# Order of evictions, forms and bank numbers in a one-core encoder layer built from seven-product blocks

## The chip, the core and the metric

The kernel runs on one core of a Trainium2 chip. The metric is device time of one execution in microseconds (us). A compared time is the median of several runs. One further execution is profiled; the traces quoted below come from it.

## The reference

One encoder layer in fp32 on 256 tokens of width 2048: a half-weighted SwiGLU feed-forward (FFN, hidden width 5632), a mixer of two attentions, a second such FFN, a gated per-token embedding and a final RMSNorm.

```python
h = h + 0.5 * swiglu(rmsnorm(h, ffn1_norm), ffn1_w_gate, ffn1_w_up, ffn1_w_down)
z = rmsnorm(h, mix_norm) @ w_in           # q|k|v, MLA latents, rope key, gate_a, gate_b
merged = sigmoid(gate_a) * (NA2D(q, k, v) @ w_branch_a) + sigmoid(gate_b) * (MLA(...) @ w_branch_b)
h = h + merged @ w_out
h = h + 0.5 * swiglu(rmsnorm(h, ffn2_norm), ffn2_w_gate, ffn2_w_up, ffn2_w_down)
h = h + sigmoid(rmsnorm(h, pl_norm) @ w_pl_gate) * (p @ w_pl)
return rmsnorm(h, final_norm)
```

## The kernel before, in words

**Products.** Every fp32 operand is held as two parts, hi (rounded by a cast on ACT) and lo (the rest, a subtraction on DVE). `split` (lines 90 and 91) makes them; `triple` (lines 95 to 97) multiplies them with three matmuls on TensorE (PE): x_lo by hi, x_hi by hi, x_hi by lo. A row "L95" or "L96" thus uses the hi tile of a weight, "L97" the lo tile.

**Granules.** All matrix products are cut into granules, kept in the list `grans` in the order in which PE works them off. The loop at the end of the file takes each granule g in turn. It first calls `convert()`, which starts coming granules' weight loads and splits as long as tiles W0 to W5 are free (a granule of an FFN needs two of them, one of a unit one), then writes the granule's matmuls, then runs the tasks that `at(d, fn)` put down for this step d granules ago, and then frees the granule's W tiles. The framework adds the semaphores; the order on each engine is the order in which the code is written (`manual_schedule`). Raw weights land in three buffers R0 to R2 by DMAs that SyncE issues.

**Units.** The mixer and the embedding are made of `Unit`s: ordinary products that add up in two PSUM banks out of B0 to B3, handed out in turn by `acc_bank` with the counter `turn["acc"]`, and evacuated by `evac`. A unit granule has 12 matmuls.

**Blocks.** The FFNs' products are `Block`s. Each computes two outputs for two token tiles (c11, c12, c21, c22) with seven products in place of eight wherever the 2x2 scheme is used (granules i in `SEVEN` = {2, 4, 6}, each in a first half `SevenA` of 9 matmuls and a second half `SevenB` of 12) and with plain products elsewhere (`Plain`, 24 matmuls). Eight banks collect partial sums q1 to q8; q1 lies in B0, q6 in B1, q7 in B2, q3 in B3, q2 in B4, q4 in B5, q5 in B6, q8 in B7 (`add`, line 218). Gate and up projections make one block per 512 hidden columns with 11 granules (i = 0 to 7); each of the three parts of the down projection makes two blocks. There are 33 blocks.

**A block's end.** The last granule is always a plain one. One step after the last `SevenB`, `early` (lines 187 to 195) gathers q1, q5, q6 and q7 on ACT and DVE. At the last granule the loop calls `late`'s two functions: `first` adds q2 and q4 (lines 201 and 202), then `convert()` writes the next weight split, then `rest` adds q8 and q3 (lines 205 and 206) and calls `done`: Silu and a product (lines 537 and 538) after a gate and up block, an addition to h (line 548, or line 550's DMA) after a down block. The next block's first granule is plain: its matmuls write B4, B5, B7 and B3 in this order, six each.

**Forms.** The activations that a block multiplies are made by `make_form`: four transposes on PE into a side bank (`bank`: B0 to B2 in turn inside the FFNs), then for a plain chunk a cast on ACT (line 385) and a subtraction on DVE that reads the bank (line 394), and for a chunk in `SEVEN` a copy to Z on ACT, four sums on DVE (line 357) and a split of 7 x 128 columns (lines 90 and 91, tile H or X, "128x896" in the profile). `hidden_forms` makes two chunks one granule after each gate and up block, `new_forms` two at each quarter of the mixer's last product. Next to the sixteen pairs in which the first chunk is in `SEVEN`, the FFNs have pairs of two plain chunks.

**Norms.** `next_stat` puts down the squares of a quarter of h (line 454, two instructions on ACT and their accumulator reads). After the last part's first down block, `added` puts them down 2 and 3 granules later.

Of the kernel before, what the change touches and what calls it, by code (L numbers as in the profile page):

```python
# [11 lines left out]
ALU = mybir.AluOpType  # L12
# [9 lines left out]
SEVEN = {2, 4, 6}  # L22
# [5 lines left out]
def encoder_kernel(ctx, tc, x, p, ffn1_norm, ffn1_w_gate, ffn1_w_up, ffn1_w_down, mix_norm, w_in,  # L28
# [11 lines left out]
    V, S, G, PE = nc.vector, nc.scalar, nc.gpsimd, nc.tensor  # L40
# [13 lines left out]
    def piece(tag, shape, dt=F32):  # L54
        return mem.tile(shape, dt, tag=tag, name=nm(tag))
# [5 lines left out]
    turn = {"acc": 0, "side": 0, "raw": 0}  # L61
# [24 lines left out]
    def at(d, fn):  # L86
        tasks.setdefault(step[0] + d, []).append(fn)

    def split(hi, lo, r):
        S.copy(hi, r)  # L90
        V.tensor_tensor(out=lo, in0=r, in1=hi.bitcast(F32), op=ALU.subtract)  # L91
# [22 lines left out]
    class Granule:  # L114
# [25 lines left out]
        def matmuls(self):  # L140
            u, k0, nk, hi, lo = self.u, self.k0, self.nk, self.hi, self.lo
            if k0 == 0:
                u.ps = [acc_bank() for _ in range(2 if u.N == 512 else 1)]
            ps = u.ps
            for k in range(nk):
                kt = k0 + k
                if u.N < 512:
                    xh, xl = u.xop(kt)
                    o = ps[0][0:u.N, 0:T]
                    PE.matmul(o, hi[:, k, :], xl, start=(kt == 0), stop=False)  # L150
                    PE.matmul(o, hi[:, k, :], xh, start=False, stop=False)
                    PE.matmul(o, lo[:, k, :], xh, start=False, stop=(kt == u.K - 1))
                    continue
                one = u.by_token and kt >= 4
                for t in range(1 if one else 2):
                    triple(ps[t], u.xtile(kt, t), hi[:, k, :], lo[:, k, :], kt == 0, kt == u.K - 1)
                if one:
                    u.kept.append((kt, hi[:, k, :], lo[:, k, :]))
            if k0 + nk == u.K:
                if not u.by_token:  # L160
                    u.evac(ps)
                    return
                u.evac(ps, 0)
                for kt, a, b in u.kept:
                    triple(ps[1], u.xtile(kt, 1), a, b, False, kt == u.K - 1)
                u.evac(ps, 1)

    def unit(*a, **k):
        Unit(*a, **k)
# [4 lines left out]
    class Block:  # L174
# [22 lines left out]
        def late(self):  # L197
            q = self.q

            def first():  # L200
                V.tensor_tensor(out=self.u, in0=q[2], in1=self.u, op=ALU.add)  # L201
                V.tensor_tensor(out=self.v, in0=q[4], in1=self.v, op=ALU.add)  # L202

            def rest():
                V.tensor_tensor(out=self.c, in0=q[8], in1=self.c, op=ALU.add)  # L205
                V.tensor_tensor(out=self.w, in0=q[3], in1=self.w, op=ALU.add)  # L206
                self.done(self.u, self.w, self.v, self.c)
            return first, rest

# [23 lines left out]
    class Plain(Pair):  # L233
# [6 lines left out]
        def matmuls(self):  # L240
            b, hi, lo = self.blk, self.hi, self.lo
            seven_on[0] = True
            f = b.form(self.i)
            for n, ws, fs in ((2, (0, 1), (1, 2)), (4, (0, 1), (0, 3)), (8, (3, 2), (0, 3)), (3, (3, 2), (1, 2))):
                for k in range(2):
                    b.add(n, f(fs[k]), hi[:, ws[k], :], lo[:, ws[k], :], self.end and k == 1)
            if self.end:
                return b.late()

    class SevenA(Pair):  # L250
# [51 lines left out]
    for nme, g in (("ffn1", ffn1_norm), ("mix", mix_norm), ("ffn2", ffn2_norm), ("pl", pl_norm),  # L302
                   ("qa", q_a_norm), ("kva", kv_a_norm)):
        n = g.shape[-1] // P
# [58 lines left out]
    def plain_tiles(src, i):  # L363

        ps = bank()
        for j, (k, t) in enumerate(((0, 1), (0, 0), (1, 0), (1, 1))):
            PE.transpose(ps[:, j * P:j * P + P], src(t, 2 * i + k), ident)  # L367
        return ps
# [6 lines left out]
    def place(where, i):  # L375
        tag, half = where[i]
        if i in SEVEN:
            return piece(tag, [P, 2, 8, P], F32R)
        if half == 0:
            shared[tag] = piece(tag, [P, 2, 2, 4, P], F32R)  # L380
        return shared[tag][:, half]
# [19 lines left out]
    def make_form(where, i, j, src, gc=None):  # L401

        ps = plain_tiles(src, j)
        f = place(where, i)
        if i not in SEVEN:
            plain_form(f, ps, gc)
            return f
        z = piece("Z", [P, 8, P])
        scaled(z[:, 0:4, :].rearrange("p a b -> p (a b)"), ps, gc)
        sums(z[:, 0:4, :], z[:, 4:8, :])  # L410
        split(f[:, 0, 1:8], f[:, 1, 1:8], z[:, 1:8, :])
        return f

    def new_forms(n, gname):
        for i in (2 * n, 2 * n + 1):
            forms[i] = make_form(XPLACE, i, i, h_tile, gcol[gname] + 2 * i)

    zs = []
# [86 lines left out]
    def next_stat(phase, n, d):  # L505
        def f():
            stat_chunk(phase, n)
            if n == 3:
                stat_done(phase)
        at(d, f)  # L510
# [5 lines left out]
    def tmps(tag):  # L516
        return [tmp.tile([P, 512], F32, tag=tag, name=nm(tag)) for _ in range(2)]


    def ffn(phase, wg, wu, wd, nxt):  # L520
        hidden = {}

        def hidden_forms(c, a, d):
            m = c % 4

            def tr(j):
                i = 2 * m + j
                hidden[i] = make_form(HPLACE, i, j, lambda t, kt: a[t][:, kt * P:kt * P + P])
            for j in range(2):
                at(d[j], lambda j=j: tr(j))  # L530

        def gated(c):
            def done(c11, c12, c21, c22):
                r, rh = rstd[phase], half[phase]
                s = tmps("s")
                for t, (g, u) in enumerate(((c11, c12), (c21, c22))):
                    S.activation(s[t], g, AF.Silu, scale=r[:, t:t + 1])  # L537
                    V.scalar_tensor_tensor(out=u, in0=u, scalar=rh[:, t:t + 1], in1=s[t],  # L538
                                           op0=ALU.mult, op1=ALU.mult)
                hidden_forms(c, [c12, c22], (1, 1))  # L540
            return done

        def added(n, final):
            def done(c11, c12, c21, c22):
                for k, t, o in ((n, 0, c11), (n, 1, c21), (n + 1, 0, c12), (n + 1, 1, c22)):
                    hs = h[:, t, k * 512:k * 512 + 512]
                    if final:
                        V.tensor_tensor(out=hs, in0=hs, in1=o, op=ALU.add)
                    else:
                        G.dma_start(hs, o, accum_op=ALU.add)  # L550
                if not final:
                    return
                if n == 0:
                    at(1, lambda: new_xT(0, nxt))
                    at(1, lambda: new_xT(1, nxt, (0,)))
                    at(2, lambda: new_xT(1, nxt, (1,)))
                    next_stat(nxt, 0, 2)
                    next_stat(nxt, 1, 3)
                else:
                    at(2, lambda: new_xT(2, nxt))  # L560
                    at(3, lambda: new_xT(3, nxt))
                    next_stat(nxt, 2, 4)
                    next_stat(nxt, 3, 5)
            return done

        hold = {}

        def gate_evac(ps):
            at(4, lambda: gate_late(ps))

        def gate_late(ps):
            r = rstd[phase]
            hold["a"] = tmps("t")
            for t in range(2):
                S.activation(hold["a"][t], ps[t], AF.Silu, scale=r[:, t:t + 1])

        def up_evac(ps):
            rh = half[phase]
            a = hold.pop("a")
            for t in range(2):  # L580
                V.scalar_tensor_tensor(out=a[t], in0=ps[t], scalar=rh[:, t:t + 1], in1=a[t],
                                       op0=ALU.mult, op1=ALU.mult)
            hidden_forms(0, a, (1, 2))

        for c0, c1 in PARTS:
            for c in range(c0, c1):
                if grans:
                    Block([rows(wg, c * 512), rows(wu, c * 512)], form_of(forms), 8, gated(c))
                else:
                    unit(rows(wg, 0), 16, 512, None, gate_evac, xtile=first_tile)  # L590
                    unit(rows(wu, 0), 16, 512, None, up_evac, xtile=first_tile)
            part = wd[c0 * 512:c1 * 512]
            for n in (0, 2):
                Block([rows(part, n * 512), rows(part, n * 512 + 512)], form_of(hidden), 2 * (c1 - c0),
                      added(n, c1 == NC_FF))
# [610 lines left out]
```

## Time and profile before

| what | value |
|---|---|
| median of 3 runs | 2188.25 us (2185.91 to 2188.34) |
| profiled execution | 2186.35 us |
| its span, first to last instruction | 2184.6 us |
| PE busy | 2153.1 us (99%) |
| DVE busy | 1720.2 us (79%) |
| ACT busy | 1128.9 us (52%) |
| mean granted TensorE clock | 0.997 of full speed |

An instruction's row in the timeline has its start and its duration in us, its engine and line, what it writes and reads, and in brackets how long the engine idled before it and who ended that. "PE" is a matmul, "PEld" the load of its stationary operand, which runs beside the matmul before it. Matmuls overlap: one is 0.39 us long but the next starts 0.23 us after it, so a delay shorter than 0.16 us shows no idle time.

### The profile page before, as it was taken

How to read it: one execution, taken by the hardware profiler on the slowest of the kernel's cores; microseconds unless marked ns; L12 is line 12 of the kernel's file. 1: busy time of each engine (PE TensorE's matmuls, PEld its weight loads, DVE VectorE, ACT ScalarE, POOL GpSimd, SP SyncE). 2: the span in 40 equal slices, each digit the busy share in tenths (PEclk: the TensorE clock that was granted, in tenths of full speed). 3: DMA queues.
4: the chain of work that ended last, by engine and by line, in shares of the span. 5: the costliest groups of instructions: out<-in, count | busy, mean ns of one | idle time of the engine just before them, and what ended most of it. 6: DMA issues, size and time to landing. Idle time of an engine off the chain costs nothing.

```text
span 2184.6 us, 25377 instructions
## 1 busy us (share of the span) xinstructions
PE 2153.1 (99%) x9693; PEld 1771.4 (81%) x9693; DVE 1720.2 (79%) x1856; ACT 1128.9 (52%) x1172; POOL 64.6 (3%) x73
## 2 busy tenths in 40 slices
PE   9999999999999999999999999999999999999998
PEld 8878888888887888888888888788888878887786
DVE  6899889998999855555655556999889998899865
ACT  6455555554555554445544445555455554555553
POOL 0000000000000000230000000000000000000000
PEclk9999999999999999999999999999999999999999
DMA  7556765567655554574455555556676647755653
GB/s 260 185 188 196 233 193 193 200 211 226 204 195 177 176 190 145 155 212 157 160 194 184 192 192 174 193 193 209 201 218 201 211 160 233 230 186 189 211 171 128
DMA packets 218026, 421.99 MB, mean 193 GB/s; under 512 B 13576, under 2 KB 14160, under 8 KB 217776
## 3 DMA queue, kind: packets, MB, share of 16 engines
q1 hardware_dynamic: 212048, 408.46, 56.3%
q0 software_dynamic: 5824, 11.89, 3.0%
q8 instruction: 76, 1.25, 0.2%
q14 instruction: 46, 0.38, 0.0%
q10 hardware_dynamic: 32, 0.01, 0.0%
HBM read 409.83 MB, written 2.10 MB: 189 GB/s over the span
## 4 chain that ended last, share of the span: by engine, by line
PE 81%; DVE 13%; issue 3%; ACT 3%; DMA 1%; DVEq 0%; POOL 0%; ACTq 0%; POOLq 0%
PE B L97 26%; PE B L95 26%; PE B L96 25%; DVE W L91 6%; ACT W L90 2%; DVE t L202 1%; DVE pt L205 1%; DVE R L257 1%; DVE Z L357 1%; DMA R<-in_w_in_dram 1%; DVE pt L538 1%; PE B L775 1%; PE B L343 1%; PE B L367 1%; DVE R L259 1%
## 5 line engine op out<-in xcount | busy, mean ns | idle before, releaser
L91 DVE TENSOR_TENSOR W<-R,W 128x1024 fp32r<-128x1024 f32 (+2 forms) x697 | 1065.2, 1546 | 321.2 <-ACT W L90 319.2
L90 ACT CAST W<-R 128x1024 fp32r<-128x1024 f32 (+2 forms) x697 | 904.4, 1310 | 709.8 <-DVE R L257 279.2
L95 PE MATMUL B<-W,X 128*128 128x512 f32 x2113 | 835.8, 396 | 8.1 <-DVE pt L206 4.2
L97 PE MATMUL B<-W,X 128*128 128x512 f32 x2113 | 825.0, 390 | 4.1 <-DVE W L91 4.1
L96 PE MATMUL B<-W,X 128*128 128x512 f32 x2113 | 823.7, 390 | 0.0
L95 PEld LDWEIGHTS B<-W,X 128*128 128x128 f32 x2113 | 397.4, 188 | 97.6 <-DVE pt L205 9.5
L97 PEld LDWEIGHTS B<-W,X 128*128 128x128 f32 x2113 | 397.2, 188 | 91.5 <-DVE W L91 7.9
L96 PEld LDWEIGHTS B<-W,X 128*128 128x128 f32 x2113 | 397.6, 188 | 80.3
L95 PE MATMUL B<-W,H 128*128 128x512 f32 x800 | 314.4, 393 | 2.7 <-DVE H L394 1.6
L97 PE MATMUL B<-W,H 128*128 128x512 f32 x800 | 312.3, 390 | 3.5 <-DVE W L91 3.5
L96 PE MATMUL B<-W,H 128*128 128x512 f32 x800 | 311.6, 389 | 0.0
L95 PEld LDWEIGHTS B<-W,H 128*128 128x128 f32 x800 | 150.2, 188 | 39.1 <-DVE pt L205 6.1
L97 PEld LDWEIGHTS B<-W,H 128*128 128x128 f32 x800 | 150.2, 188 | 37.5 <-DVE W L91 6.0
L96 PEld LDWEIGHTS B<-W,H 128*128 128x128 f32 x800 | 150.3, 188 | 30.4
L257 DVE TENSOR_TENSOR R<-R 128x1024 f32<-128x1024 f32 x95 | 116.4, 1225 | 3.3
L260 DVE TENSOR_TENSOR R<-R 128x512 f32<-128x512 f32 x95 | 65.8, 692 | 3.2
L259 DVE TENSOR_TENSOR R<-R 128x512 f32<-128x512 f32 x95 | 65.8, 692 | 3.3
L550 POOL DMA_DIRECT2D h<-t x16 | 14.1, 1018 | 1410.5 <-DVE t L201 1186.6
L385 ACT COPY Z<-B 128x512 f32<-128x512 f32 x16 | 9.4, 586 | 67.4 <-PE B L367 67.4
L90 ACT CAST H<-Z 128x896 fp32r<-128x896 f32 x16 | 15.1, 943 | 53.9 <-DVE Z L357 53.9
L537 ACT ACTIVATE s<-t,sm 128x512 f32<-128x512 f32 x42 | 28.1, 717 | 26.4 <-DVE t L201 26.4
L385 ACT CAST H<-B 128x512 fp32r<-128x512 f32 x28 | 15.8, 584 | 30.7 <-PE B L367 30.7
(207 smaller groups left out, 1047.1 us busy)
## 6 DMA issues: line engine op xcount, KB each, us to landing
R<-in_ffn_w_down_dram SPq DMA_DIRECT2D x176, 512.0 KB, 5.4
R<-in_ffn_w_gate_dram SPq DMA_DIRECT2D x170, 512.0 KB, 3.7
R<-in_ffn_w_up_dram SPq DMA_DIRECT2D x168, 512.0 KB, 4.9
R<-in_w_in_dram SPq DMA_DIRECT2D x64, 1024.0 KB, 5.2
R<-in_w_out_dram SPq DMA_DIRECT2D x16, 1024.0 KB, 5.0
R<-in_w_pl_gate_dram SPq DMA_DIRECT2D x16, 1024.0 KB, 5.1
R<-in_w_branch_a_dram SPq DMA_DIRECT2D x8, 1024.0 KB, 4.9
R<-in_w_branch_b_dram SPq DMA_DIRECT2D x8, 1024.0 KB, 5.0
```

Source lines behind the costliest of these rows:

```text
L90: S.copy(hi, r)
L91: V.tensor_tensor(out=lo, in0=r, in1=hi.bitcast(F32), op=ALU.subtract)
L95: PE.matmul(o, xl, hi, start=start, stop=False)
L96: PE.matmul(o, xh, hi, start=False, stop=False)
L97: PE.matmul(o, xh, lo, start=False, stop=stop)
L202: V.tensor_tensor(out=self.v, in0=q[4], in1=self.v, op=ALU.add)
L205: V.tensor_tensor(out=self.c, in0=q[8], in1=self.c, op=ALU.add)
L257: V.tensor_tensor(out=raw[:, 0:4:3, :], in0=raw[:, 0:3:2, :], in1=raw[:, 3:4, :].to_broadcast([P, 2, 512]), op=ALU.add)
L259: V.tensor_tensor(out=raw[:, 2, :], in0=raw[:, 0, :], in1=raw[:, 2, :], op=ALU.add)
L260: V.tensor_tensor(out=raw[:, 1, :], in0=raw[:, 2, :], in1=raw[:, 1, :], op=ALU.add)
L385: S.copy(o, ps)
L537: S.activation(s[t], g, AF.Silu, scale=r[:, t:t + 1])
```

## The change

In `late`, `first` now adds all four sums, q8 and q3 too, ahead of `convert()`, and `rest` only calls `done`. When the last granule of a block is written, the bank counter for units goes back to 0. In `make_form`, the split of a `SEVEN` chunk's form is put off by one granule. In `new_forms` and in `hidden_forms`, the plain chunk of a pair comes first. In `added`, the squares of the first two quarters of h move from 2 and 3 granules to 5 and 6 granules after the last part's first down block.

```diff
             def first():
                 V.tensor_tensor(out=self.u, in0=q[2], in1=self.u, op=ALU.add)
                 V.tensor_tensor(out=self.v, in0=q[4], in1=self.v, op=ALU.add)
-
-            def rest():
                 V.tensor_tensor(out=self.c, in0=q[8], in1=self.c, op=ALU.add)
                 V.tensor_tensor(out=self.w, in0=q[3], in1=self.w, op=ALU.add)
+
+            def rest():
                 self.done(self.u, self.w, self.v, self.c)
             return first, rest
...
             if self.end:
+                turn["acc"] = 0
                 return b.late()
...
         sums(z[:, 0:4, :], z[:, 4:8, :])
-        split(f[:, 0, 1:8], f[:, 1, 1:8], z[:, 1:8, :])
+        at(1, lambda: split(f[:, 0, 1:8], f[:, 1, 1:8], z[:, 1:8, :]))
         return f
...
-        for i in (2 * n, 2 * n + 1):
+        for i in sorted((2 * n, 2 * n + 1), key=lambda i: i in SEVEN):
...
-            for j in range(2):
+            for j in sorted((0, 1), key=lambda j: 2 * m + j in SEVEN):
                 at(d[j], lambda j=j: tr(j))
...
-                    next_stat(nxt, 0, 2)
-                    next_stat(nxt, 1, 3)
+                    next_stat(nxt, 0, 5)
+                    next_stat(nxt, 1, 6)
```

No instruction is added or taken away on any engine. On DVE, this is the end of the seventh gate and up block of FFN 1 (near 400 us in the trace of before) and the two granules behind it, before; B4, B5, B7, B3 are q2, q4, q8, q3, R raw weights, W their split, Z and H forms:

```order
L201 TENSOR_TENSOR t_445_2992<-B4_408_2713,t_445_2992 128x512
L202 TENSOR_TENSOR t_446_2993<-B5_409_2720,t_446_2993 128x512
L91 TENSOR_TENSOR W3_451_3007<-R0_449_3003,W2_450_3006 128x2048
L205 TENSOR_TENSOR pt_448_2995<-B7_410_2727,pt_448_2995 128x512
L206 TENSOR_TENSOR pt_447_2994<-B3_411_2734,pt_447_2994 128x512
...
L260 TENSOR_TENSOR R1_454_3018<-R1_454_3018 128x512
L357 TENSOR_TENSOR Z_463_3062<-Z_463_3062 128x128 x4
L91 TENSOR_TENSOR H2_462_3061<-Z_463_3062,H2_462_3061 128x896
L394 TENSOR_TENSOR H4_416_2760<-B2_464_3070,H4_416_2760 128x512
L91 TENSOR_TENSOR W1_466_3078<-R1_454_3018,W0_465_3077 128x2x512
L91 TENSOR_TENSOR W1_466_3078<-R1_454_3018,W0_465_3077 128x1024
L91 TENSOR_TENSOR W3_469_3111<-R2_467_3107,W2_468_3110 128x2048
```

The same stretch of DVE in the changed kernel, where most line numbers are one higher:

```order
L201 TENSOR_TENSOR t_445_2992<-B4_408_2713,t_445_2992 128x512
L202 TENSOR_TENSOR t_446_2993<-B5_409_2720,t_446_2993 128x512
L203 TENSOR_TENSOR pt_448_2995<-B7_410_2727,pt_448_2995 128x512
L204 TENSOR_TENSOR pt_447_2994<-B3_411_2734,pt_447_2994 128x512
L91 TENSOR_TENSOR W3_451_3009<-R0_449_3005,W2_450_3008 128x2048
...
L261 TENSOR_TENSOR R1_454_3018<-R1_454_3018 128x512
L395 TENSOR_TENSOR H4_413_2746<-B1_461_3056,H4_413_2746 128x512
L358 TENSOR_TENSOR Z_464_3069<-Z_464_3069 128x128 x4
L91 TENSOR_TENSOR W1_466_3076<-R1_454_3018,W0_465_3075 128x2x512
L91 TENSOR_TENSOR W1_466_3076<-R1_454_3018,W0_465_3075 128x1024
L91 TENSOR_TENSOR H2_463_3068<-Z_464_3069,H2_463_3068 128x896
L91 TENSOR_TENSOR W3_469_3111<-R2_467_3107,W2_468_3110 128x2048
```

The two sums that read B7 and B3 moved ahead of one weight split; the plain form's subtraction (H4) moved ahead of the sums in Z; the split of H2 moved behind the two of W1 but still stands ahead of that of W3.

On PE, this is the first unit of the embedding (its weights are in W1) right behind the last block's last matmul, before:

```order
L97 MATMUL B3_2257_14761<-W5_2286_14921,H4_2175_14228 128x512
L95 MATMUL B3_2297_15002<-W1_2288_14935,X0_2258_14768 128x512
L96 MATMUL B3_2297_15002<-W1_2288_14935,X0_2258_14768 128x512
L97 MATMUL B3_2297_15002<-W1_2288_14935,X0_2258_14768 128x512
L95 MATMUL B0_2298_15003<-W1_2288_14935,X0_2258_14768 128x512
```

And in the changed kernel:

```order
L97 MATMUL B3_2257_14761<-W5_2284_14917,H4_2172_14214 128x512
L95 MATMUL B0_2297_15002<-W1_2288_14935,X0_2258_14768 128x512
L96 MATMUL B0_2297_15002<-W1_2288_14935,X0_2258_14768 128x512
L97 MATMUL B0_2297_15002<-W1_2288_14935,X0_2258_14768 128x512
L95 MATMUL B1_2298_15003<-W1_2288_14935,X0_2258_14768 128x512
```

The unit's two banks were B3 and B0 and are now B0 and B1. PE's order is otherwise the same, but for the two chunks of a pair, whose transposes change places.

## The prediction, made before the changed kernel was run

> **What bounds the kernel now.** I read the page first, then what PE waited for, then PE's timeline around one wait of each kind, then the DVE and ACT rows that those waits hang on.
>
> ```profile
> span 2184.6 us, 25377 instructions
> ...
> PE 2153.1 (99%) x9693; PEld 1771.4 (81%) x9693; DVE 1720.2 (79%) x1856; ACT 1128.9 (52%) x1172; POOL 64.6 (3%) x73
> ```
>
> PE is busy for 2153.1 of 2184.6 us, so it sets the time, and an edit that moves no PE work can only take waits out of it. The view of PE's waits names them:
>
> ```profile
> PE B L97 <- DVE W L91: 7.6, 15, 1.0
> PE B L95 <- DVE pt L206: 4.2, 1, 4.2
> PE B L95 <- DVE H L394: 4.1, 5, 0.9
> ```
>
> That is 16 us. It isn't all, because matmuls overlap. PE's timeline just behind a block's end:
>
> ```profile
> 402.32 0.39 PE L97 MATMUL B<-W,X 128*128 128x512 f32 x1
> 402.79 0.50 PE L95 MATMUL B<-W,X 128*128 128x512 f32 x1
> 403.13 0.40 PE L96 MATMUL B<-W,X 128*128 128x512 f32 x1
> 403.37 0.40 PE L97 MATMUL B<-W,X 128*128 128x512 f32 x1
> ```
>
> No idle time is shown, yet three steps take 403.37 - 402.32 = 1.05 us where three of 0.23 take 0.69: 0.36 us are lost. The view of line 205 (q8's sum, once per block), under who waited for it (us, times):
>
> ```profile
>   PEld B L95: 15.6, 31
> ```
>
> So 31 of 33 block ends hold up the weight load of the first matmul into q8's bank. The Trainium skill ("Perfetto Trace Analysis", the note at its head) calls matmul busy time a bad metric because matmuls are pipelined. This trace agrees: by busy time and idle rows 16 us could go, by starts twice as much (below).
>
> **Part 1, four sums in a row: 31 waits go.** DVE at the same block's end:
>
> ```profile
> 398.65 0.68 DVE L201 TENSOR_TENSOR t<-B,t 128x512 f32<-128x512 f32 x1
> 399.25 0.68 DVE L202 TENSOR_TENSOR t<-B,t 128x512 f32<-128x512 f32 x1
> 399.85 2.28 DVE L91 TENSOR_TENSOR W<-R,W 128x2048 fp32r<-128x2048 f32 x1
> 402.05 0.69 DVE L205 TENSOR_TENSOR pt<-B,pt 128x512 f32<-128x512 f32 x1
> ```
>
> The weight split of 2.28 us stands between the four sums, of which two in a row are 0.60 apart; L206 follows L205 like that. L205 ends at 402.74 and PE goes on at 402.79. With the split behind, q8's sum starts at 399.85 and ends at 400.53, 2 us before PE wants its bank (402.55), and q3's ends at 401.13. Gain: 31 x 0.36 = 11.2 us. The price: the split starts 1.20 later and ends at 403.33 in place of 402.13. Its first use on PE:
>
> ```profile
> 407.03 0.39 PE L97 MATMUL B<-W,X 128*128 128x512 f32 x1
> ```
>
> 4.9 us of cover before, 407.03 - 0.36 - 403.33 = 3.3 after: nothing. Behind it on DVE stand L538's products, which need Silu and wait for the same total of DVE work as before, so the transposes and `done` come no later. The raw buffer comes free 1.2 us later; SyncE's load into it serves a split three granules on, over 10 us later, and a load takes about 5. Nothing there. POOL's DMA additions (line 550) stay behind the same split.
>
> **Part 2, forms.** All sixteen hidden pairs with a `SEVEN` chunk end in one wait on PE each, eleven like this and five for line 394:
>
> ```profile
> 412.04 0.39 PE L95 MATMUL B<-W,X 128*128 128x512 f32 x1
> ...
> 417.03 0.39 PE L96 MATMUL B<-W,X 128*128 128x512 f32 x1
> 417.77 0.50 PE L97 MATMUL B<-W,X 128*128 128x512 f32 x1 [0.35 <-DVE W L91]
> 418.11 0.40 PE L95 MATMUL B<-W,X 128*128 128x512 f32 x1
> 418.35 0.40 PE L96 MATMUL B<-W,X 128*128 128x512 f32 x1
> ```
>
> Three steps from 417.03 take 1.32 in place of 0.69: a shown idle of 0.35 costs 0.63, so idle plus 0.28. The 15 waits for L91 are these eleven, three long ones (part 3) and one at the kernel's start, which stays; (7.6 - 0.4 - 3.0) / 11 gives 0.38 each, so 11 x 0.65 = 7.2 us. The five for L394, whose row stands above, cost 4.1 + 5 x 0.28 = 5.5 us. Both hang on this stretch of DVE and ACT:
>
> ```profile
> 409.15 1.01 DVE L357 TENSOR_TENSOR Z<-Z 128x128 f32<-128x128 f32 x4
> 411.23 1.09 DVE L91 TENSOR_TENSOR H<-Z,H 128x896 fp32r<-128x896 f32 x1 [1.06 <-ACT H L90]
> 412.23 0.69 DVE L394 TENSOR_TENSOR H<-B,H 128x512 fp32r<-128x512 f32 x1
> 412.83 2.35 DVE L91 TENSOR_TENSOR W<-R,W 128x1024 fp32r<-128x1024 f32 x2
> 415.42 3.96 DVE L91 TENSOR_TENSOR W<-R,W 128x2048 fp32r<-128x2048 f32 x2 [0.23 <-ACT W L90]
> ```
>
> ```profile
> 410.25 0.94 ACT L90 CAST H<-Z 128x896 fp32r<-128x896 f32 x1 [3.33 <-DVE Z L357]
> ```
>
> The sums wait for nobody, ACT's cast waits for the sums, DVE idles 1.06 for the cast, and the weight casts stand behind it on ACT. With the plain form first and the split put off: L394 runs 409.0 to 409.7 (its bank is read 3 us sooner, so the five waits for a side bank go), the sums 409.6 to 410.6, the two splits of W1 410.5 to 412.9 (their casts need only L257 and L260, done by 409.1), the split of H 412.8 to 413.9 (cast meanwhile). The next weight cast needs PE to leave its tile, at about 412.0 - 0.4; 1.9 long, it ends near 413.8. Its L91 then runs 413.9 to 416.2, against 415.42 to 417.71. PE, 0.36 sooner, wants it at 417.26 - 0.36 = 416.9. All sixteen waits go, 12.7 us, with 0.7 us to spare. DVE's work up to there is the same; only the idle 1.06 and 0.23 go. The late split of H is needed five granules later or more: free.
>
> **Part 3, the three long waits.**
>
> ```profile
> 709.74 0.50 PE L97 MATMUL B<-W,H 128*128 128x512 f32 x1 [0.93 <-DVE W L91]
> ```
>
> ```profile
> 1371.67 0.50 PE L97 MATMUL B<-W,X 128*128 128x512 f32 x1 [1.02 <-DVE W L91]
> ```
>
> ```profile
> 2051.34 0.50 PE L97 MATMUL B<-W,H 128*128 128x512 f32 x1 [1.01 <-DVE W L91]
> ```
>
> With 0.28 each, 3.8 us. The one at 1371 is a form behind the mixer: the same reordering leaves about 0.3 of it (PE also comes no earlier there); 1.0 goes. The other two follow the first down block of the last part, where the squares stand ahead of the weight cast:
>
> ```profile
> 2045.84 0.63 ACT L454 ACTIVATE sq<-h 128x512 f32<-128x512 f32 x1
> ...
> 2047.06 1.90 ACT L90 CAST W<-R 128x2048 fp32r<-128x2048 f32 x1
> ```
>
> Without them the cast starts 1.22 sooner: about 1.1 of each 1.3 goes. But they now stand ahead of a later cast, whose L91 (the first of three from 2058.98, 2.29 long, so to 2061.27) was just in time:
>
> ```profile
> 2058.98 4.57 DVE L91 TENSOR_TENSOR W<-R,W 128x2048 fp32r<-128x2048 f32 x3 [0.58 <-ACT W L90]
> ```
>
> ```profile
> 2061.70 0.39 PE L97 MATMUL B<-W,H 128*128 128x512 f32 x1
> ```
>
> 0.43 to spare before. The price lies between 0 (the squares fit in ACT's idle time) and 1.22 + 0.28 = 1.5; I take 0.7, nearer the row with its small margin. Sum of part 3: 1.0 + 2 x (1.1 - 0.7) = 1.8 us.
>
> **Part 4, banks of the embedding's first unit.**
>
> ```profile
> 2066.46 0.39 PE L97 MATMUL B<-W,H 128*128 128x512 f32 x1
> 2071.01 0.76 PE L95 MATMUL B<-W,X 128*128 128x512 f32 x1 [4.16 <-DVE pt L206]
> ```
>
> ```profile
> 2071.01:2076.03 5.02, 5.02 (x12) 3.96 (x13) 2.26 (x4) 0.00 (x0) 0.00 (x0) 0.53 0.38 140
> ```
>
> The unit began in B3, which L206 leaves last. PE lost 4.55 - 0.23 = 4.32 us, and then 12 matmuls took 5.02 in place of 2.76 at a granted clock of 0.53: 2.26 more, 6.6 in all. B0 and B1 are read out by `early`, before 2066. What comes next: after two granules of 12 matmuls (2066.7 + 5.4 = 2072.1) PE transposes h, and needs the second of these additions:
>
> ```profile
> 2070.78 1.28 DVE L548 TENSOR_TENSOR h<-h,t 128x512 f32<-128x512 f32 x2
> ```
>
> They end at 2072.06 in either order of the sums, so PE, somewhat early there, may wait 0.4. Gain 6.2 us, between 5.1 and 6.6.
>
> **Sum.** 11.2 + 12.7 + 1.8 + 6.2 = 31.9 us. The profiled execution took 2186.35 us (span 2184.6 and 1.75 around it): 2154.5. The runs' median, 2188.25, is 1.9 above it, which gives 2156.3. I say 2155. A measurement of this kernel can tell about 0.2%, 4.4 us, from no change.
>
> **Rivals.** *The forms' waits stay* (14%). The split of H still stands ahead of the L91 that was late. If the 0.7 us to spare isn't there (ACT's cast later than I walked it), the sixteen waits stay or come back one granule later: 31.9 - 12.7 = 19.2, 2167. For it: DVE's work before that L91 is unchanged. Against: the 1.06 of idle in front of the H split has no cause left.
>
> *The embedding still waits* (6%): if a sum of the last block stays in the unit's way in spite of the reset, four sums in a row alone bring the last one from 2070.86 to about 2068.6, and PE waits 2.1 in place of 4.3; with the slow stretch kept, 31.9 - 6.2 + 2.2 = 27.9, 2158.5. The Trainium skill ("TensorE: Matmul & The Clock Gate", "What's actually happening") has the half clock follow an idle window of about 3.4 us; by it the slow stretch would go with a wait of 2.1, and this case would end 2.3 lower. The granted 0.53 behind a 4.16 us wait and none behind waits of 1 us agree with that page; no run here shows one between.
>
> *Slower: the weight split is the late one* (2%). Place: the L91 behind the four sums, at all 33 ends. If its 4.9 us of cover weren't real (the tile wanted sooner than the L97 row says), each end would pay the 1.20 + 0.28 in place of 0.36: 33 x 1.48 = 49 against 31.9, 2204. It decides against the change once the loss per end passes 31.9 / 33 = 0.97, that is with under 0.6 us of cover. The 407.03 row speaks against it.
>
> *No effect* (1%): something off this list limits PE.
>
> My forecast has 77%. Its own range is 2150 (all 34.3 us that parts 1 to 4 list as lost go, and a run as low as 2185.91) to 2160 (part 3 at 1.5, embedding at 5.1). The range to hold it 8 times in 10 reaches on to the first rival: 2149 to 2168. Faster 0.97, same 0.01, slower 0.02.
>
> **What would show it.** In the changed profile, PE's waits should have no row for line 394 (now 395), no 4.2 us wait, and no loads waiting for the sum of q8; the granted clock should not fall near 2040. L91 on H should have no idle in front of it. At most short waits for L91 should stay: one at the start, one behind the mixer, and two in the last down blocks, now behind the squares. The sum of starts lost should fall from about 34 to 3 us. I'm wrong if waits for L91 of W are still fifteen, or if new ones follow the block ends.

## The result and the profile after

| | kernel before | changed kernel |
|---|---|---|
| median of 4 runs | 2188.3 us (2185.91 to 2188.83) | 2154.36 us (2151.62 to 2156.39) |
| profiled execution | 2186.35 us | 2156.39 us |
| its span | 2184.6 us | 2154.7 us |

The ratio of after to before is 0.9846, 95% interval 0.9829 to 0.9863: faster by 1.5%. The predicted 2155 is 0.6 us off. By the medians the gain is 33.9 us, between the two traces 29.9. As will be seen, the closeness is partly luck: the trace gained 35 us where 31.9 were expected, and lost 5 us at a place that the prediction didn't look at.

The page of after, its span and its engines:

```profile
span 2154.7 us, 25398 instructions
...
PE 2138.3 (99%) x9693; PEld 1774.8 (82%) x9693; DVE 1716.2 (80%) x1856; ACT 1137.0 (53%) x1172; POOL 62.9 (3%) x73
```

PE's waits in after (us in total, times, longest):

```profile
PE B L847 <- DVE t L840: 3.1, 2, 2.9
PE B L1121 <- POOL ident L293: 1.4, 1, 1.4
PE B L97 <- DVE W L91: 0.8, 2, 0.5
PE B L95 <- DVE X L336: 0.2, 1, 0.2
```

Fifteen waits for L91 have become two (one at the kernel's start, 0.53 us, as predicted, and one in the last down blocks, 0.27), the rows for H and for q3's sum (pt) are gone, and the first row is a wait that the prediction doesn't have.

The other comparisons go by the starts of the same matmuls in both traces. PE's timeline of after at the block end whose rows before were 402.32 to 403.37:

```profile
395.40 0.39 PE L97 MATMUL B<-W,X 128*128 128x512 f32 x1
395.63 0.39 PE L95 MATMUL B<-W,X 128*128 128x512 f32 x1
395.86 0.39 PE L96 MATMUL B<-W,X 128*128 128x512 f32 x1
396.08 0.39 PE L97 MATMUL B<-W,X 128*128 128x512 f32 x1
```

Three steps take 0.68 us in place of 1.05: 0.37 gained, and 0.37 to 0.42 at nearly every other end. DVE in after at that end:

```profile
391.73 0.68 DVE L201 TENSOR_TENSOR t<-B,t 128x512 f32<-128x512 f32 x1
392.33 0.68 DVE L202 TENSOR_TENSOR t<-B,t 128x512 f32<-128x512 f32 x1
392.93 0.68 DVE L203 TENSOR_TENSOR pt<-B,pt 128x512 f32<-128x512 f32 x1
393.53 0.68 DVE L204 TENSOR_TENSOR pt<-B,pt 128x512 f32<-128x512 f32 x1
394.12 2.28 DVE L91 TENSOR_TENSOR W<-R,W 128x2048 fp32r<-128x2048 f32 x1
...
402.03 0.68 DVE L395 TENSOR_TENSOR H<-B,H 128x512 fp32r<-128x512 f32 x1
402.63 1.02 DVE L358 TENSOR_TENSOR Z<-Z 128x128 f32<-128x128 f32 x4
403.56 2.35 DVE L91 TENSOR_TENSOR W<-R,W 128x1024 fp32r<-128x1024 f32 x2
405.84 1.08 DVE L91 TENSOR_TENSOR H<-Z,H 128x896 fp32r<-128x896 f32 x1
406.84 3.95 DVE L91 TENSOR_TENSOR W<-R,W 128x2048 fp32r<-128x2048 f32 x2
```

q8's sum (L203) ends at 393.61, 2.0 us before its bank is wanted at 395.63. Below the dots stands the stretch of the forms: no row has idle time in front, where before the split of H had 1.06 and that of W 0.23.

PE of after where the embedding begins, its last matmul on H and its first on X, and then the same place in the windows view (us; busy time and count of PE, PEld, DVE, ACT and POOL; granted clock; DMA share; GB/s):

```profile
2043.01 0.39 PE L97 MATMUL B<-W,H 128*128 128x512 f32 x1
2043.24 0.39 PE L95 MATMUL B<-W,X 128*128 128x512 f32 x1
```

```profile
2043.24:2046.00 2.76, 2.76 (x14) 2.29 (x13) 2.76 (x5) 0.00 (x0) 0.00 (x0) 1.00 1.01 410
```

The wait of 4.16 us is gone, and the granted clock behind it is 1.00 where it was 0.53.

**The new wait.** PE in after, in the mixer:

```profile
924.37 0.39 PE L97 MATMUL B<-W,X 128*128 128x512 f32 x1
927.63 0.47 PE L847 MATMUL B<-ident,t 128*128 128x128 f32 x1 [2.87 <-DVE t L840]
928.29 1.76 PE L847 MATMUL B<-ident,t 128*128 128x128 f32 x7 [0.18 <-DVE t L840]
929.70 0.78 PE L95 MATMUL B<-W,X 128*128 128x512 f32 x1
930.27 0.63 PE L96 MATMUL B<-W,X 128*128 128x512 f32 x1
930.70 0.63 PE L97 MATMUL B<-W,X 128*128 128x512 f32 x1
```

The same place before, with PE 11 us later:

```profile
938.77 0.33 PE L846 MATMUL B<-ident,t 128*128 128x128 f32 x1 [0.44 <-DVE t L839]
939.43 0.98 PE L846 MATMUL B<-ident,t 128*128 128x128 f32 x7 [0.33 <-DVE t L839]
940.17 0.48 PE L95 MATMUL B<-W,X 128*128 128x512 f32 x1
```

Compared by starts, after loses 3.1 us up to the first matmul behind the transposes and 1.9 more behind it, where matmuls are 0.43 apart in place of 0.23. The windows view puts the granted clock at half there:

```profile
929.70:933.69 3.99, 3.99 (x12) 3.12 (x10) 2.04 (x1) 1.65 (x3) 3.08 (x2) 0.50 0.76 230
```

The chain behind it, DVE and then ACT in after:

```profile
925.06 1.86 DVE L91 TENSOR_TENSOR W<-R,W 128x1024 fp32r<-128x1024 f32 x1 [4.27 <-ACT W L90]
926.84 1.40 DVE L840 TENSOR_SCALAR t<-B,sm 128x512 f32<-128x512 f32 x2
```

```profile
916.64 1.06 ACT L90 CAST W<-R 128x1024 fp32r<-128x1024 f32 x1 [1.67 <-PE B L97]
923.98 1.99 ACT L90 CAST W<-R 128x1024 fp32r<-128x1024 f32 x2 [6.28 <-DMA R<-in_w_in_dram]
```

The transposes want L840's result; L840 stands on DVE behind a weight split, that behind ACT's cast, and the cast waits 6.28 us for a weight load. Before, the cast waited 4.48 us for its load:

```profile
935.75 2.00 ACT L90 CAST W<-R 128x1024 fp32r<-128x1024 f32 x2 [4.48 <-DMA R<-in_w_in_dram]
```

Where the load's time went is shown by POOL in after, and by the windows view of that time:

```profile
902.84 8.27 POOL L822 DMA_DIRECT2D H<-in_na_rpb_dram  x12 [196.09 <-PE B L776]
```

```profile
902.00:910.00 8.00, 8.00 (x37) 6.65 (x36) 3.58 (x4) 3.64 (x4) 7.16 (x11) 1.00 1.03 238
910.00:918.00 8.00, 8.00 (x37) 6.63 (x36) 5.01 (x3) 3.17 (x3) 6.41 (x8) 1.00 1.04 221
918.00:926.00 8.00, 6.76 (x30) 5.25 (x28) 3.73 (x3) 1.99 (x2) 7.75 (x5) 1.00 1.03 269
```

POOL puts down 16 loads of the attention bias (na_rpb) one behind the other, and the DMA engines are full for 24 us at 221 to 269 GB/s, against 410 at the same share in the embedding's row above. The tile view of R gives the time from issue to landing of the weight loads between 900 and 930:

```profile
DMA to landing us min/median/max: 5.1/8.3/15.8
```

The burst itself isn't new: before has the same 16 loads, from 916.41 on, and its longest weight load there took 14.0 us. What differs is how late the one load comes that the cast waits for, 4.48 us there and 6.28 here, and that one more split on DVE behind it takes 1.86 us in place of 1.22.

### The profile page after: what moved, and what is told of

Read it like the earlier page. It is cut to its first block, busy times and chain, and to the rows that moved or that the text cites. A ratio compares the mean times of both kernels' runs of the same rounds, so it can differ in the third digit from the quotient of the medians.

```text
span 2154.7 us, 25398 instructions
## 1 busy us (share of the span) xinstructions
PE 2138.3 (99%) x9693; PEld 1774.8 (82%) x9693; DVE 1716.2 (80%) x1856; ACT 1137.0 (53%) x1172; POOL 62.9 (3%) x73
## 3 DMA queue, kind: packets, MB, share of 16 engines
q8 instruction: 76, 1.25, 0.2%
## 4 chain that ended last, share of the span: by engine, by line
PE 97%; DVE 1%; DMA 1%; ACT 0%; issue 0%; POOL 0%; DVEq 0%; ACTq 0%; POOLq 0%
PE B L97 31%; PE B L95 31%; PE B L96 31%; PE B L368 1%; DMA R<-in_w_in_dram 1%; PE B L776 1%; PE B L344 0%; DVE W L91 0%; PE B L762 0%; PE B L800 0%; PE B L883 0%; PE B L801 0%; ACT W L90 0%; PE B L847 0%; PE B L1121 0%
## 5 line engine op out<-in xcount | busy, mean ns | idle before, releaser
L91 DVE TENSOR_TENSOR W<-R,W 128x1024 fp32r<-128x1024 f32 (+2 forms) x697 | 1066.4, 1548 | 318.4 <-ACT W L90 315.9
L538 ACT ACTIVATE s<-t,sm 128x512 f32<-128x512 f32 x42 | 28.1, 717 | 31.9 <-DVE t L201 31.9
L539 DVE SCALAR_TENSOR_TENSOR pt<-pt,sm,s 128x512 f32<-128x512 f32 x42 | 29.5, 744 | 0.0
L332 ACT ACTIVATE X<-B,gT 128x256 fp32r<-128x256 f32 x40 | 15.7, 478 | 25.3 <-PE B L344 25.3
```

## Experiments

e1 to e4 do one part of the change each on the kernel before; e5 and e6 split the part on forms; the others start from the changed kernel.

**e1: the sums alone.**

```diff
                 V.tensor_tensor(out=self.v, in0=q[4], in1=self.v, op=ALU.add)
-
-            def rest():
                 V.tensor_tensor(out=self.c, in0=q[8], in1=self.c, op=ALU.add)
                 V.tensor_tensor(out=self.w, in0=q[3], in1=self.w, op=ALU.add)
+
+            def rest():
                 self.done(self.u, self.w, self.v, self.c)
```

> The four sums in a row alone, on the kernel before. Additive theory (each part takes out its own waits): 31 weight-load waits of about 0.39 us go, 12 us, and the embedding's wait of 4.2 shrinks by 2.3: 2174. Coupled theory (DVE's chain from a block's end to the late weight split is as long as before, so PE that arrives 0.39 sooner waits 0.39 longer at the next late split): the gain stays only at the 13 of 31 ends that no form wait and no squares wait follows, 5 us, plus 2.3 at the embedding, about 2181; the sixteen waits behind forms grow by 0.35 to 0.4 each.

Measured: 2177.76 us against 2187.35, ratio 0.9955 (0.9941 to 0.997). The block ends give 0.37 to 0.41 each. At the sixteen form waits 0.14 to 0.24 is lost again each time, about half: PE comes 0.39 sooner, but what it waits for on DVE comes only about 0.2 sooner. The wait that was 0.35 at 417.77 is now 0.53 long:

```profile
415.52 0.50 PE L97 MATMUL B<-W,X 128*128 128x512 f32 x1 [0.53 <-DVE W L91]
```

So the truth lies between the two cases expected. At the embedding, the timeline and the windows view of e1:

```profile
2061.70 0.47 PE L95 MATMUL B<-W,X 128*128 128x512 f32 x1 [1.92 <-DVE pt L204]
```

```profile
2061.70:2064.40 2.70, 2.70 (x12) 2.22 (x13) 2.70 (x4) 0.00 (x0) 0.00 (x0) 1.00 1.00 387
```

The wait is 1.92 in place of 4.16, and twelve matmuls behind it take 2.70 us at full clock: the sums alone take 4.4 of the 6.6 us there.

**e2: forms alone** (plain chunk first, and the split late).

```diff
-        split(f[:, 0, 1:8], f[:, 1, 1:8], z[:, 1:8, :])
+        at(1, lambda: split(f[:, 0, 1:8], f[:, 1, 1:8], z[:, 1:8, :]))
...
-        for i in (2 * n, 2 * n + 1):
+        for i in sorted((2 * n, 2 * n + 1), key=lambda i: i in SEVEN):
...
-            for j in range(2):
+            for j in sorted((0, 1), key=lambda j: 2 * m + j in SEVEN):
```

> Plain chunk first and split put off, alone, on the kernel before. Additive theory: sixteen waits (11 x 0.69 and 5 x 1.1) and most of the one behind the mixer go, 14 us, to 2174; the 31 waits for the sum of q8 stay as they are. Coupled theory: the same 2174, since these waits come after the block's end and nothing behind them is late; the parts then add up to less than the whole, the rest showing only when both are in.

Measured: 2174.68 us against 2187.35, ratio 0.9946 (0.9931 to 0.9961). All sixteen waits go, 0.66 to 0.71 us for the eleven and 1.07 to 1.23 for the five, and 1.31 at 1371. The block ends keep theirs; two kinds of row of e2's waits, PEld and PE:

```profile
PEld B L95 <- DVE pt L205: 15.3, 31, 0.5
...
PE B L846 <- DVE t L839: 3.3, 2, 3.1
```

The second row is the mixer's wait again, on a kernel that has neither the sums nor the banks changed; its trace loses 5.2 us there.

**e3: the bank counter alone.**

```diff
             if self.end:
+                turn["acc"] = 0
                 return b.late()
```

> The bank counter's reset alone, on the kernel before. Both theories: the 4.16 us wait at the embedding's start goes and the slow stretch behind it too, 6.2 to 6.6 us, 2182, and nothing else changes. If only the wait went and the stretch stayed: 4.3, 2184.

Measured: 2180.93 us against 2187.35, ratio 0.997 (0.9961 to 0.998). In the trace 4.32 us of wait and 2.30 us of slow matmuls go at the embedding, 6.6 in all. The ten times of e3 lie in two groups, 2179.06 to 2179.69 and 2182.18 to 2183.42; the profiled execution, 2183.42, is of the upper one and loses 3.85 us in the mixer (a wait of 2.70, then slow matmuls).

**e4: the squares alone.**

```diff
-                    next_stat(nxt, 0, 2)
-                    next_stat(nxt, 1, 3)
+                    next_stat(nxt, 0, 5)
+                    next_stat(nxt, 1, 6)
```

> The squares three granules later alone, on the kernel before. The waits of 0.93 and 1.01 us in the last down blocks shrink by about 0.9 each and a wait of 0 to 0.5 us for a later weight split comes up instead: 1 to 2 us, 2187, hardly to be told from no change by time; the trace decides. Rival: the squares only move the wait, no change.

Measured: 2186.43 us against 2187.35, ratio 0.9994 (0.9985 to 1.0004). The time can't tell it from nothing. The trace shows the two waits go (1.19 and 1.25) and a new one at the later cast each time (0.56 and 0.65), about 1.2 us net at these places; 0.7 is lost again at the embedding's start, whose wait is 0.21 longer with more slow matmuls behind it.

**e5: the plain chunk first, alone.** Only the two `sorted` lines of e2.

> The plain chunk of a pair first, with the split of the other form where it was, on the kernel before. If the waits for the late weight split come from DVE's idle 1.06 us between the sums and the form's split, the eleven stay (7.5 us) and only the five for line 394 go and the same places now wait for the weight split instead, 0.3 to 0.5 each: a gain of about 3, 2184. If the order of the two chunks does all the work: as with both edits, 2174.

Measured: 2189.14 us against 2186.74, ratio 1.0003 (0.9994 to 1.0012). The two medians alone would give 1.0011, but the times of both kernels lie in two groups some 3 us apart (below), and a median falls into one of them; the ratio goes by all runs. PE's waits in e5:

```profile
PE B L97 <- DVE W L91: 11.7, 20, 1.0
```

The five waits for L394 are gone (1.07 to 1.23 gained each), but twenty waits for L91 stand where fifteen did: 0.84 to 0.92 is lost again about 5 us behind each of the five places, in a wait of 0.51 to 0.60 where 0.3 to 0.5 was expected, and the eleven others grow by 0.09 to 0.17. The five places keep 1.3 us together and the eleven lose 1.4, so plain first alone gains nothing, and the 3 us expected didn't come.

**e6: the late split alone.** Only the first edit of e2.

> The split of a form put off by one granule, with the chunks in their old order, on the kernel before. If the idle 1.06 us is the cause, all sixteen waits and most of the one behind the mixer go with this edit alone, 13 to 14 us, 2174: line 394 comes right behind the four sums and so 2 us sooner, in time for its bank, and plain first adds nothing. If both edits are needed: the five waits for line 394 stay (5 us), 2179.

Measured: 2173.51 us against 2186.74, ratio 0.9939 (0.9922 to 0.9955). PE's waits in e6:

```profile
PE B L95 <- DVE pt L206: 4.2, 1, 4.2
PE B L846 <- DVE t L839: 2.6, 2, 2.3
PE B L97 <- DVE W L91: 2.4, 3, 1.0
PE B L1120 <- POOL ident L292: 1.4, 1, 1.4
```

All sixteen go, and the one at 1371: there is no row for L394, and of fifteen waits for L91 three are left. The deferral does the whole of part 2.

**The changed kernel once more, with e7 to e9.**

> The changed kernel once more, unedited, to see whether the wait in the mixer (2.9 us on PE for line 840 and 1.9 us of slow clock behind it) belongs to the change or to the execution. If to the change: again 5 us in the profile. If to the execution: anything from 0.6 to 6, as in the other profiles so far; 2154 either way.

Measured: 2155.27 us against 2188.66 on that chip, ratio 0.9851 (0.9835 to 0.9867). The mixer's wait is 2.3 us this time; its trace loses 1.8 us less there than the first one.

**e7: the bias loads in fours.** POOL puts down four bias loads, then the two selects on them, which wait until they have landed, then the next four; the number of loads and selects is the same.

```diff
                                     bass.AP(tensor=na_rpb.tensor, offset=na_rpb.offset + (7 - r + i) * 31 + 15 - 63,
                                             ap=[[1, 64], [465, 8], [1, 64]]))
-                for r in range(4):
                     q = M["bias"][r // 2][64 * (r % 2):64 * (r % 2) + 64].rearrange("p a i c -> p (a i) c")
```

> The changed kernel with the sixteen loads of the bias table in four groups of four, each behind the two selects of the group before on POOL, in place of all sixteen at once. If the loads crowd out the weight load that the mixer's wait hangs on: the wait and the slow stretch go, 1 to 5 us by execution, about 2151.5. If the selects are the cause (they run beside DVE splits that take 2 to 3 us in place of 1.2): no change, 2154.

Measured: 2150.59 us (2150.07 to 2150.82) against 2188.66, ratio 0.9829 (0.9814 to 0.9843). POOL in e7, and the landing times of the weight loads between 900 and 930:

```profile
903.45 2.82 POOL L822 DMA_DIRECT2D H<-in_na_rpb_dram  x4 [196.16 <-PE B L776]
911.54 1.69 POOL L826 TENSOR_SCALAR_AFFINE_SELECT H<-H 64x1536 f32<-64x1536 f32 x1 [5.27 <-DMA H<-in_na_rpb_dram]
```

```profile
DMA to landing us min/median/max: 5.4/5.8/6.7
```

The longest load takes 6.7 us in place of 15.8. PE has no wait for t in e7 any more, and beside the first trace of after it gains 4.3 us up to the transposes and 1.9 behind them. Pacing the loads thus takes the wait away. But the edit also moves the selects, which lie between the loads now, so the burst is the likely cause, and a share of POOL's selects that run beside DVE isn't excluded.

**e8: the sums behind the weight split.** The two calls at a block's end change places, so that the split stands ahead of all four sums.

```diff
-            more[0]()
             convert()
+            more[0]()
             more[1]()
```

> The changed kernel with all four sums behind the weight split in place of ahead of it. The next block's first matmul then waits for q2's sum: it ends 2.29 us later, about 2.3 us behind a block's natural end where the matmul wants it 0.5 us earlier than that, so about 1.8 to 2.0 us per end at 32 ends, 60 us: 2214. If the ends had cover left (PE filled from elsewhere), less than half of it.

Measured: 2215.71 us against 2188.66, ratio 1.0127 (1.0106 to 1.0147). PE's waits in e8:

```profile
PE B L95 <- DVE t L201: 51.1, 30, 2.0
```

By starts 31 ends lose 1.9 to 2.0 us each against after (one of them 2.25). The order of four sums and one split, with the same work on every engine, is worth 60 us from one end to the other; before stood with the split in the middle.

**e9: squares later still**, at 9 and 10 granules, with e7's edit.

```diff
-                    next_stat(nxt, 0, 5)
-                    next_stat(nxt, 1, 6)
+                    next_stat(nxt, 0, 9)
+                    next_stat(nxt, 1, 10)
```

> The kernel with the paced bias loads, and the squares at 9 and 10 granules (in the unit behind the blocks) in place of 5 and 6. If the squares cause the waits that are left in the last down blocks (0.23 and 0.54 us) and the late start of the next unit's transposes: another 0.8 to 1.3 us, about 2150.5. If not, the same time as with the paced loads alone.

Measured: 2149.75 us (2149.5 to 2149.85) against 2188.66, ratio 0.9825 (0.981 to 0.984). PE's waits in e9:

```profile
PE B L97 <- DVE W L91: 0.2, 1, 0.2
PE B L95 <- DVE X L336: 0.2, 1, 0.2
```

The waits behind the squares are gone (the L91 row left is the kernel's start); by starts that is 0.25 us at the first place and 0.57 at the second, and 0.17 at the transposes of h that follow. This is the fastest version tried, 0.3% below the changed kernel, nearly all of it from e7's edit.

## Why the prediction was right, and where it was off

The gain of each term, by the starts of the same matmuls in the first trace of after:

| term | predicted us | measured us |
|---|---|---|
| part 1, 31 block ends | 11.2 | 12.2, less 0.65 given back at two places |
| part 2, sixteen forms | 12.7 | 13.2 (eleven 7.6, five 5.6) |
| part 3, three long waits | 1.8 | 3.0 |
| part 4, banks of the embedding | 6.2 | 6.5 |
| start of the kernel | 0 | 0.6 |
| mixer's transposes | 0 | -5.0 |
| everything else | 0 | under 0.1 |
| sum | 31.9 | 29.9 (2184.6 - 2154.7) |

**Part 1** held, by its reason and nearly by its size: an end is worth 0.39 in place of 0.36, because the block's first granule lost a little more than the three steps that the prediction counted. What the walk left out is that PE then comes sooner at places that have nothing to do with blocks: 0.44 went at the side bank that waits for L336 (the last row of after's waits), 0.21 behind the first down block's end near 2022. The price of the split behind the sums was put at nothing; no wait follows a block's end in after, so the 3.3 us of cover held, and with it the slower rival fell. e8 shows the sign of the order: the split ahead of all four sums costs 1.9 to 2.0 us an end.

**Part 2** came out near its size, and the walk held on the way: DVE enters that block's end 6.9 us earlier (L201 at 391.73 against 398.65), and that much earlier than in the walk its times came within 0.2 us (the split of H at 405.84, against 412.8 - 6.9 = 405.9; that of W at 406.84, against 407.0). But the prediction credited the five waits for L394 to the plain form going first, since its bank is read sooner. e5 and e6 show that step to be wrong in its cause: plain first alone only moves those five waits on, to the next L91, and the late split alone removes all sixteen. What made all sixteen late was one thing, the 1.06 us that DVE idled in front of the split of H, with what stood behind it: L394 at five places, L91 of W at eleven. The rival that the forms' waits stay fell with it.

**Part 3** was mis-sized: 1.28 of the wait at 1371 went where 1.0 was expected, since nothing of it is left; the two in the last down blocks gave 1.2 and 1.3 where 1.1 was taken; and the squares' new wait cost 0.25 and 0.57 us where 0.7 was taken for each. The new wait stands where it was predicted, behind the squares at the L91 that had little to spare (the matmul at 2061.70 before):

```profile
2038.12 0.50 PE L97 MATMUL B<-W,H 128*128 128x512 f32 x1 [0.27 <-DVE W L91]
```

The e4 run paid 0.56 and 0.65 for the same two. e9 takes these waits away.

**Part 4** held: the wait of 4.16 and the slow stretch behind it went together, and of the 0.4 us allowed for the transposes of h 0.17 was lost. The second rival (a wait of about 2 at the embedding, were a sum left in the way) didn't happen in after, but e1 made just that wait. It was priced with the slow stretch kept; in e1 that stretch went, so the 2158.5 should have been 2.2 lower. The Trainium skill ("TensorE: Matmul & The Clock Gate", "What's actually happening"), whose idle window of about 3.4 us would have had it so, was right there; its figure did not hold elsewhere, below.

**What the prediction missed** is the mixer. Its before-trace had the mixer's wait with 0.8 us in all and the prediction didn't price it. What decides its size isn't settled. It was short (longest 0.4 to 1.0) in the traces of before, e4 and e5, and 2.3 to 3.1 in those of e1, e2, e3, e6, e8 and both of after; but e3 differs from before only in banks, and its ten times stand in two groups 3.5 us apart, as if single executions had it or not. Three things fit that. With the bias loads in fours the runs of e7 lie within 0.75 us and those of e9 within 0.35, while the runs of before on that chip stand in two groups, three from 2184.87 to 2186.25 and four from 2188.66 to 2189.59. The ten times of e5, a kernel as fast as before, do the same: three from 2185.46 to 2185.90, the traced one with its short wait among them, and seven from 2188.24 to 2189.75. And where the trace loses 3.8 us or more in the mixer (e2, e3, e8 and the first of after), the traced execution is the slowest of its kernel's runs. So part of what the table books against the change is likely a matter of the execution: without the 5.0 us the profiled 2156.39 would have been 2151.4, and the fastest run of after took 2151.62. That only the profiled executions show the place, and the others only their time, leaves this argued and not shown.

**Do the parts add up?** With the mixer left out, the traces gain 13.6 (e1), 15.1 (e2) and 6.8 us (e3), and e4 about 1.2 at its own places, 36.7 together. The embedding is in this twice, 4.4 us in e1 beside 6.6 in e3; and the 0.14 to 0.24 us that e1 loses again at each of sixteen forms, 2.9 in all, come back once the forms' waits are gone. That makes 36.7 - 4.4 + 2.9 = 35.2, against 29.9 + 5.0 = 34.9 in after. Nothing finer than about 1 us can be read from this: the slow stretch at the embedding alone is 0.6 us longer in e2 than in before, and 0.6 shorter in e5 and e6, which leave that place as it was.

## What to carry to other kernels

Where the bounding engine is 99% busy, compare the starts of the same instructions: of 35 us gained here, about half were never shown as idle time. Of several jobs due at once on a helper engine, put first the one that the bounding engine needs first (here sums that free a bank, ahead of a weight split with 5 us of cover), and keep a job that waits for another engine (the split of H behind ACT's cast) behind those that are ready. Before settling the sum, look also at the waits that are small in the one trace at hand but hang on a transfer: here that was the price that differed most from trace to trace.

## What was not expected of the hardware

Sixteen bias loads of 128 KB put down one behind the other filled the DMA engines for 24 us at 221 to 269 GB/s, and weight loads of 1 MB that take 5.4 to 6.7 us beside four of them took up to 15.8.

The granted clock halves after shorter idle times than expected. Idle time of PE in one piece, and what the 128x512 matmuls behind it then lost: 1.92 us, nothing (e1, embedding); in the mixer 2.30, 0.8 (e6); 2.34, 0.6 (the second trace of after); 2.53, nothing (e1); 2.70, 1.4 (e3); 2.87, 1.9 (the first of after); 3.07, 1.9 (e2); 3.08, 1.0 (e8); at the embedding 4.16 to 4.37, 1.7 to 2.9 (before, e2, e4, e5, e6). In e6, behind 4.19 us at the embedding, the first four steps from matmul to matmul were still 0.23 to 0.31 us, and only then came seven of 0.43: the slow stretch needn't begin where the wait ends. The Trainium skill ("TensorE: Matmul & The Clock Gate", "What's actually happening") puts the window at about 3.4 us and lets it run freely; the idle times of 2.3 to 3.1 are shorter than that and had the clock down in six traces of seven, and that 2.53 left it up while 2.30 did not agrees with a window whose place is not fixed.
